# Four pairs of k tiles by seven products in gate and up, bank copies on ACT, and one sum of weights on GpSimd

## The chip, the cores and the metric

The kernel runs on one core of one Trainium2 chip. The metric is device time in microseconds of one execution, the median of several runs. The engines are PE (TensorE, matrix products), ACT (ScalarE), DVE (VectorE), POOL (GpSimd) and SP (SyncE, which here only issues DMAs). Every engine takes its own instructions in a fixed order and waits on semaphores for the others.

## The reference, cut to what matters

Two decoder layers on 256 tokens of width 2048: sparse attention in layer a, dilated window attention in layer b, both with attention to 256 memory tokens, and after each a SwiGLU feed-forward network (FFN) of width 5632. All inputs are float32. The change is in the FFN and in what prepares its input:

```python
D_MODEL, SEQ, D_FF = 2048, 256, 5632

def swiglu(h, w_gate, w_up, w_down):
    return (jax.nn.silu(h @ w_gate) * (h @ w_up)) @ w_down

# at the end of each layer
h = h + o                                    # output projection of the attention
return h + swiglu(rms_norm(h, norm_ffn), w_gate, w_up, w_down)
```

## The kernel before

**Precision.** Every product of two float32 matrices is made of three PE matmuls. ACT rounds an operand to a high part (`hi`, line 76) and DVE forms the low part as the difference (`lo`, line 77); `mm3` (lines 83 to 87) adds hi·hi, lo·hi and hi·lo into a PSUM bank of 128x512. Below, a *product* is one `mm3`: three matmuls of 128x128 by 128x512. Weights are split on the chip as they arrive: `whi`/`wlo` for a *plain* chunk (128x1024, line 105, three buffers each), `qhi`/`qlo` for a *quarter* (line 865, two buffers each).

**Pairs of k tiles by seven products.** A group of the FFN makes four banks: two token tiles by two column blocks of 512 (gate and up, or two blocks of down). Two k tiles and these two by two form a 2x2 by 2x2 block product, which needs eight products when done plainly. The kernel does it by the Winograd form of Strassen's scheme in seven. `NPR = 3` pairs (six k tiles) go this way in every group, the other k tiles are plain. For the three pairs together a quarter of the weights is one tile of 128x1536: q11, q12, q22, q21. Sums of activations are formed once, when the input is turned (`Paired.finish`, line 272, slots 4 to 7), sums of weights in every group by DVE (lines 886, 893, 901, 913).

**Steps of a group.** `Group.steps` (line 877) returns s0 to s6, one `product` (line 864) of a quarter or a sum of quarters each: s0 q11, s1 q11+q12, s2 q11+q12+q22, s3 q12+q22, s4 q21, s5 q21 plus the sum of three, s6 q22. Each step splits its quarter (ACT, then DVE) and issues one `mm3` for each pair. Between them `keep` (line 872) copies a bank to SBUF on ACT, and DVE adds such copies to banks (896, 898) or forms the remainder `rest` (904), which is added to the fourth bank at the end (line 980, or to `h` in line 1004). The quarters stand in four rotating buffers (line 860).

**Order of the work.** `run_groups` (line 939) writes PE's order by hand: the steps of the *next* group lie between the plain chunks of the *present* one. `spacing` (line 932) says how many plain chunks stand before each step: with ten plain chunks in a group 2, 1, 1, 2, 1, 2, 1. When the last plain chunk is issued, `done` reads the four banks: for gate and up `gate_up` (line 977: Silu on ACT, a product on DVE, then eight transposes on PE and splits in `heads`, issued some products later), for down an addition to `h`. ACT, DVE, SP and POOL are ordered by the scheduler of the language; only PE's order is fixed by the program. Bank 3 has one PSUM buffer, banks 0 to 2 have two (line 69).

**Groups.** An FFN has eleven gate-and-up groups of 16 k tiles; the first is wholly plain (64 products), the other ten have 21 + 40 = 61 products. They lie in portions of 4, 4 and 3 (line 26), each followed by two down groups (16, 16 and 12 k tiles); the last portion of layer b goes through `final` (line 1159) instead. So there are 20 paired gate-and-up groups and 10 paired down groups in all.

The input of the FFN is turned by `Paired.turn` (line 282) while `project_out` (line 812) runs. GpSimd raises to the power -1/2 in `finish_rstd` (line 213) and does little else.

Of the kernel before, what the change touches and what calls it, by code (L numbers as in the profile page):

```python
# [16 lines left out]
P = 128  # L17
# [9 lines left out]
NPR = 3  # L27
NSL = 8
NRK = KT - 2 * NPR
SW = NPR * NSL * P  # L30
XW = SW + NRK * T
QW = NPR * 512
WARM = 9
EPS = 1e-6
# [7 lines left out]
def decoder_trunk(ctx: ExitStack, tc: tile.TileContext, a: dict, out: bass.AP):  # L42
# [7 lines left out]
    work = ctx.enter_context(tc.tile_pool(name="work", bufs=1))  # L50
    work.tile([P, 20], F32, name="padw")
    phase = ctx.enter_context(ExitStack())
    aux_stack = ExitStack()
    fbufs = [1]
    fpool = mm_ps = aux_ps = mm_tags = None
# [132 lines left out]
    ac = phase.enter_context(tc.tile_pool(name="ac", bufs=1))  # L188
# [3 lines left out]
    peT = ac.tile([P, 2, 32], F32, name="peT")  # L192
    gbias = ac.tile([P, 36], F32, name="gbias")
    w2 = ac.tile([P, 2, 2, HD], F32, name="w2")
    ac.tile([P, 16], F32, name="pada")
# [20 lines left out]
    def square_sum(ssq, src):  # L216
        junk = work.tile([P, 512], F32, tag="rope2", name="junk")
        nc.scalar.activation(junk, src, AF.Square, accum_out=ssq)  # L218
# [31 lines left out]
    class Paired:  # L250
# [4 lines left out]
        def __init__(self, x, nk, gain=None, sums=True):  # L255
            self.gain, self.sums, self.nk = gain, sums, nk
            self.S = tuple(v[:, :SW].rearrange("p (q s t) -> p q s t", s=NSL, t=P) for v in x)
            self.R = tuple(v[:, SW:].rearrange("p (k t) -> p k t", t=T) for v in x)
            self.xs = [self.at(k) for k in range(nk)]

        def at(self, k):
            if k >= 2 * NPR:
                return cols(tuple(v[:, k - 2 * NPR, :] for v in self.R))
            return lambda tt: self.slot(k // 2, ((1, 0), (2, 3))[k % 2][tt])
# [4 lines left out]
        def new_f(self):  # L269
            return fpool.tile([P, 4, P], F32, tag="xf", name="xf", bufs=fbufs[0])  # L270

        def finish(self, q, f):
            split(self.S[0][:, q, :4, :], self.S[1][:, q, :4, :], f)
            if self.sums:
                s = fpool.tile([P, 4, P], F32, tag="xs", name="xs", bufs=1)
                nc.vector.tensor_sub(s[:, 0, :], f[:, 0, :], f[:, 3, :])
                nc.vector.tensor_sub(s[:, 2, :], f[:, 1, :], f[:, 0, :])
                nc.vector.tensor_sub(s[:, 1, :], s[:, 0, :], f[:, 1, :])
                nc.vector.tensor_add(s[:, 3, :], f[:, 2, :], s[:, 1, :])
                split(self.S[0][:, q, 4:, :], self.S[1][:, q, 4:, :], s)  # L280

        def turn(self, nb, k2):
            k = nb * 4 + k2 * 2
            if k >= 2 * NPR:
                to_xT(nb, k2, None, self.gain, tuple(v[:, k - 2 * NPR:k - 2 * NPR + 2, :].rearrange("p c t -> p (c t)") for v in self.R))
                return
# [3 lines left out]
            f = self.new_f()  # L290
            for i in range(2):
                nc.scalar.activation(f[:, i * 2:i * 2 + 2, :], ps[:, i * T:(i + 1) * T].rearrange("p (s t) -> p s t", t=P),
                                     AF.Copy, scale=self.gain(k + i))
            self.finish(k // 2, f)

        def heads(self, j, tok):

            np_ = min(max(NPR - 2 * j, 0), 2)
            fs = []

            def step(tt):
# [3 lines left out]
                pv = ps.rearrange("p (c t) -> p c t", t=P)  # L305
                for q in range(np_):
                    if tt == 0:
                        fs.append(self.new_f())
                    d = fs[q][:, 1:3, :] if tt == 0 else fs[q][:, 0:4:3, :]
                    nc.scalar.activation(d, pv[:, 2 * q:2 * q + 2, :], AF.Copy)  # L310
                    if tt == 1:
                        self.finish(2 * j + q, fs[q])
                if np_ < 2:
                    r0 = 4 * j + 2 * np_ - 2 * NPR
                    n = 4 - 2 * np_
                    d = tuple(v[:, r0:r0 + n, tt * P:(tt + 1) * P] for v in self.R)
                    split(d[0], d[1], pv[:, 2 * np_:, :])
# [132 lines left out]
    att = (p1, 2, 4)  # L450

# [148 lines left out]
    def compress(kv, toks):  # L600
# [30 lines left out]
        def turn():  # L631
# [4 lines left out]
            z = ac.tile([P, 2, 60], F32, tag="cz", name="cz", bufs=1)  # L636
            nc.scalar.activation(z.rearrange("p i m -> p (i m)"), tr[:, :120], AF.Copy)
            s = ac.tile([P, 2, 30], F32, tag="cs", name="csg", bufs=1)
# [173 lines left out]
    def project_out(name, nk, ready, gi):  # L812
        op = Paired(new_x(), KT, lambda k: gains[:, gi, k:k + 1])
# [25 lines left out]
    class Group:  # L839
# [3 lines left out]

        late = False

        def __init__(self, op, quarters, rest, done, rest_done=None):
# [3 lines left out]
            self.k0 = 0 if quarters is None else 2 * NPR  # L850
# [8 lines left out]
        def load(self, i):  # L859
            t = fq.tile([P, QW], F32, tag="quart", name=("q11", "q12", "q22", "q21")[i], bufs=4)  # L860
            nc.sync.dma_start(t, self.q[i])
            return t

        def product(self, b, s, t, side, start=False):
            hl = [fq.tile([P, QW], F32R, tag=n, name=n, bufs=2) for n in ("qhi", "qlo")]
            split(hl[0], hl[1], t)
            for q in range(NPR):
                mm3(self.bank[b], self.op.slot(q, s), tuple(v[:, q * 512:(q + 1) * 512] for v in hl),
                    start and q == 0, q == NPR - 1, True)
                side.tick()  # L870

        def keep(self, b):
            t = fq.tile([P, 512], F32, tag="keep", name="keep", bufs=3)
# [3 lines left out]
        def steps(self, side):  # L877
            def s0():
                self.q11 = self.load(0)
                self.new(0)  # L880
                self.product(0, 1, self.q11, side, True)
                self.p1 = self.keep(0)

            def s1():
                self.q12 = self.load(1)
                nc.vector.tensor_add(self.q11, self.q11, self.q12)
                self.new(2)
                self.product(2, 4, self.q11, side, True)
                self.p5 = self.keep(2)

            def s2():
                self.q22 = self.load(2)
                nc.vector.tensor_add(self.q11, self.q11, self.q22)
                b2 = self.new(1)
                self.product(1, 5, self.q11, side, True)
                nc.vector.tensor_add(b2, b2, self.p1)
# [3 lines left out]
            def s3():  # L900
                nc.vector.tensor_add(self.q12, self.q12, self.q22)
                self.product(1, 6, self.q12, side)
                self.r = fq.tile([P, 512], F32, tag="rest", name="rest", bufs=2)
# [4 lines left out]
            def s4():  # L908
                self.q21 = self.load(3)
                self.product(0, 2, self.q21, side)  # L910

            def s5():
                nc.vector.tensor_add(self.q21, self.q21, self.q11)
                self.product(1, 3, self.q21, side)

            def s6():
                self.product(2, 7, self.q22, side)

            return [s0, s1, s2, s3, s4, s5, s6]

        def plain(self, c, side):
            if c == 0:
                self.new(3)
            ws = load_w(self.rest[c], 512)
            last = c == len(self.rest) - 1
            k = self.k0 + c
            for b in ((3, 0, 1, 2) if last else (0, 1, 2, 3)):
                x = self.op.xs[k](b % 2)
                mm3(self.bank[b], x, ws[b // 2], c == 0 and (b == 3 or self.k0 == 0), last, True)
# [33 lines left out]
    def ffn(pre, op, f_r, last):  # L963
        gq, gs = a[pre + "_gu_q"], a[pre + "_gu_s"]
        groups = []
        for pi, (b0, b1) in enumerate(PORTIONS):
# [4 lines left out]
            def hop(pi=pi, nk=nk, final=final, hp=hp):  # L971
                if "op" not in hp:
                    x = pair(lambda i: fh.tile([P, XW], F32R, tag=("hThi", "hTlo")[i], name=("hThi", "hTlo")[i]))
                    hp["op"] = Paired(x, nk, sums=not (final and pre == "b"))
# [346 lines left out]
```

## Time and profile before

| | |
|---|---|
| median of 3 runs | 2042.54 us (2041.19 to 2043.21) |
| the profiled execution | 2041.91 us |
| its span, first to last instruction | 2040.1 us |
| mean granted TensorE clock | 0.998 |
| busy ACT, DVE, POOL | 58%, 80%, 1% |
| from HBM | 394.87 MB, mean 196 GB/s |

The profile is one execution taken by the hardware profiler. Its *groups* name an instruction by its line, its engine and its tiles (output, an arrow, inputs), with a count, the sum of busy time and the mean of one in ns. The *waits* say who waited for whom: total us, times, longest. The *timeline* has a start, a duration, the engine, the line and the tiles, and in brackets how long the engine had stood idle and whom it waited for. The duration of a PE matmul is modelled and overlaps the next one; what a matmul costs is read from the distance of the starts. A DMA's time runs from issue to landing.

### The profile page before, as it was taken

How to read it: one execution, taken by the hardware profiler on the slowest of the kernel's cores; microseconds unless marked ns; L12 is line 12 of the kernel's file. 1: busy time of each engine (PE TensorE's matmuls, PEld its weight loads, DVE VectorE, ACT ScalarE, POOL GpSimd, SP SyncE). 2: the span in 40 equal slices, each digit the busy share in tenths (PEclk: the TensorE clock that was granted, in tenths of full speed). 3: DMA queues.
4: the chain of work that ended last, by engine and by line, in shares of the span. 5: the costliest groups of instructions: out<-in, count | busy, mean ns of one | idle time of the engine just before them, and what ended most of it. 6: DMA issues, size and time to landing. Idle time of an engine off the chain costs nothing.

```text
span 2040.1 us, 25602 instructions
## 1 busy us (share of the span) xinstructions
PE 2020.5 (99%) x9417; PEld 1676.7 (82%) x9417; DVE 1641.4 (80%) x2118; ACT 1190.4 (58%) x1573; POOL 10.8 (1%) x32
## 2 busy tenths in 40 slices
PE   9999999999999999999999999999999999999998
PEld 7898888878888888888887888878888888888886
DVE  6767898678888888888887678778888888888755
ACT  7755566656555566555565555656555565655543
POOL 0000000000000000000000000000000000000000
PEclk9999999999999999999999999999999999999999
DMA  8767633566655656556663755476556655566464
GB/s 302 270 201 236 218 116 122 178 253 199 208 184 194 201 195 225 186 186 208 203 209 114 235 167 158 147 262 201 185 186 201 225 202 186 182 206 221 136 204 146
DMA packets 104541, 400.74 MB, mean 196 GB/s; under 512 B 12128, under 2 KB 12512, under 8 KB 104032
## 3 DMA queue, kind: packets, MB, share of 16 engines
q1 hardware_dynamic: 103392, 395.31, 58.5%
q0 software_dynamic: 736, 2.75, 0.4%
q8 instruction: 74, 1.21, 0.3%
q10 hardware_dynamic: 288, 1.05, 0.1%
q14 instruction: 51, 0.42, 0.1%
HBM read 394.87 MB, written 4.19 MB: 196 GB/s over the span
## 4 chain that ended last, share of the span: by engine, by line
PE 95%; DVE 2%; ACT 1%; issue 0%; DMA 0%; SPq 0%; DVEq 0%; POOLq 0%; POOL 0%; ACTq 0%
PE mm L85 30%; PE mm L87 30%; PE mm L86 30%; PE aux L304 1%; PE aux L226 1%; DVE wlo L77 1%; PE aux L87 1%; PE aux L86 1%; PE aux L85 1%; PE aux L339 0%; ACT whi L76 0%; PE cmp L625 0%; PE cmp L624 0%; DVE E L377 0%; DMA memT_raw<-in_memT_dram 0%
## 5 line engine op out<-in xcount | busy, mean ns | idle before, releaser
L76 ACT ACTIVATE whi<-raw 128x1024 fp32r<-128x1024 f32 (+1 forms) x476 | 498.4, 1047 | 502.5 <-PE mm L86 461.3
L77 DVE TENSOR_TENSOR wlo<-raw,whi 128x1024 fp32r<-128x1024 f32 (+1 forms) x476 | 573.1, 1205 | 203.9 <-ACT whi L76 202.6
L85 PE MATMUL mm<-whi,xhi 128*128 128x512 f32 (+1 forms) x1376 | 537.5, 391 | 2.9 <-ACT junk L218 1.1
L87 PE MATMUL mm<-wlo,xhi 128*128 128x512 f32 (+1 forms) x1376 | 530.5, 386 | 0.0
L86 PE MATMUL mm<-whi,xlo 128*128 128x512 f32 (+1 forms) x1376 | 529.7, 385 | 0.0
L77 DVE TENSOR_TENSOR qlo<-q,qhi 128x1536 fp32r<-128x1536 f32 x210 | 368.6, 1757 | 75.5 <-ACT qhi L76 74.2
L76 ACT ACTIVATE qhi<-q 128x1536 fp32r<-128x1536 f32 x210 | 311.8, 1486 | 137.8 <-PE mm L86 115.2
L87 PEld LDWEIGHTS mm<-wlo,xhi 128*128 128x128 f32 x1376 | 258.3, 188 | 52.6
L85 PEld LDWEIGHTS mm<-whi,xhi 128*128 128x128 f32 x1376 | 258.6, 188 | 51.0 <-issue 2.5
L86 PEld LDWEIGHTS mm<-whi,xlo 128*128 128x128 f32 x1376 | 258.8, 188 | 47.0
L85 PE MATMUL mm<-whi,hThi 128*128 128x512 f32 x464 | 182.0, 392 | 0.1
L86 PE MATMUL mm<-whi,hTlo 128*128 128x512 f32 x464 | 180.7, 389 | 0.9 <-DVE hTlo L77 0.9
L87 PE MATMUL mm<-wlo,hThi 128*128 128x512 f32 x464 | 180.8, 390 | 0.0
L87 PE MATMUL mm<-qlo,xhi 128*128 128x512 f32 x420 | 163.5, 389 | 0.0
L85 PE MATMUL mm<-qhi,xhi 128*128 128x512 f32 x420 | 163.5, 389 | 0.0
L86 PE MATMUL mm<-qhi,xlo 128*128 128x512 f32 x420 | 163.5, 389 | 0.0
L80 DVE SCALAR_TENSOR_TENSOR wlo<-raw,gains,whi 128x512 fp32r<-128x512 f32 x160 | 113.8, 747 | 47.0 <-ACT whi L79 46.8
L79 ACT ACTIVATE whi<-raw,gains 128x512 fp32r<-128x512 f32 x160 | 107.7, 716 | 58.9 <-PE mm L86 51.3
L85 PE MATMUL mm<-whi,ohi 128*128 128x512 f32 x256 | 102.7, 401 | 1.3 <-ACT whi L79 1.3
L86 PEld LDWEIGHTS mm<-whi,hTlo 128*128 128x128 f32 x464 | 87.2, 188 | 19.0 <-DVE hTlo L77 1.2
L85 PEld LDWEIGHTS mm<-whi,hThi 128*128 128x128 f32 x464 | 87.1, 188 | 18.1 <-ACT hThi L76 0.6
L87 PEld LDWEIGHTS mm<-wlo,hThi 128*128 128x128 f32 x464 | 87.1, 188 | 18.1
(279 smaller groups left out, 2480.0 us busy)
## 6 DMA issues: line engine op xcount, KB each, us to landing
raw<-in_a_gu_s_dram SPq DMA_DIRECT2D x100, 512.0 KB, 4.2
raw<-in_b_gu_s_dram SPq DMA_DIRECT2D x100, 512.0 KB, 3.6
q<-in_a_gu_q_dram SPq DMA_DIRECT2D x40, 768.0 KB, 5.4
q<-in_b_gu_q_dram SPq DMA_DIRECT2D x40, 768.0 KB, 5.7
raw<-in_a_dn_s_dram SPq DMA_DIRECT2D x52, 512.0 KB, 4.2
raw<-in_b_dn_s_dram SPq DMA_DIRECT2D x40, 512.0 KB, 4.3
q<-in_a_dn_q_dram SPq DMA_DIRECT2D x24, 768.0 KB, 5.7
raw<-in_a_w_out_dram SPq DMA_DIRECT2D x32, 512.0 KB, 3.6
```

The source lines that it names most:

```text
L76: nc.scalar.activation(hi, src, AF.Copy)
L77: nc.vector.tensor_sub(lo, src, hi.bitcast(F32))
L79: nc.scalar.activation(hi, src, AF.Copy, scale=gain)
L80: nc.vector.scalar_tensor_tensor(lo, src, gain, hi.bitcast(F32), op0=ALU.mult, op1=ALU.subtract)
L85: nc.tensor.matmul(o, l[0], r[0], start=start, stop=False, skip_group_check=more)
L86: nc.tensor.matmul(o, l[1], r[0], start=False, stop=False, skip_group_check=more)
L87: nc.tensor.matmul(o, l[0], r[1], start=False, stop=stop, skip_group_check=more)
L226: nc.tensor.transpose(ps[:, i * P:(i + 1) * P], s, ident)
L304: nc.tensor.transpose(ps[:, i * P:(i + 1) * P], tok[tt][:, i * P:(i + 1) * P], ident)
```

## The change

Gate and up take four pairs (`NPX = 4`) instead of three, so a group has 28 + 32 = 60 products, eight plain chunks, and quarters of 128x2048. Down stays at three pairs (`NPH = 3`).

- **Buffers of the quarters:** q11, q22 and q12 get one buffer each (`qa`, `qc`, `qb`), and q21 is loaded into the buffer of q12.
- **Steps:** the sums are accumulated in place. s4 is now the product of q22, s5 loads q21, has GpSimd add it to the sum of three, and makes that product; s6 is the product of q21.
- **Bank copies:** s0 writes bank 1, ACT copies it to bank 0, and s2 goes on accumulating in bank 1. The DVE addition of line 896 and one `keep` go. In gate and up `rest` is copied by ACT into bank 3 (`begin`) before the first plain chunk accumulates there; the addition of line 980 goes.
- **Spacing:** 2, 1, 1, 2, 0, 2, 0 plain chunks for groups of eight, other rows for 16, 10 and 6, and `done` comes before s5 where it came before s6.
- **Input and heads:** `finish` works on one or two pairs at a time and forms the sums in place; `heads` copies for two pairs at once.
- **Space:** `work` goes into the phase pools, `hb` has two buffers, `keep` two, `rest` one, and some small tiles move to another pool, with padding.

```diff
-NPR = 3
+NPX = 4
+NPH = 3
-QW = NPR * 512
+QW = NPX * 512
...
+        def finish(self, q, n, f):
+            def part(s):
+                d = tuple(v[:, q:q + n, s:s + 4, :].rearrange("p q s t -> p q (s t)") for v in self.S)
+                split(d[0], d[1], f.rearrange("p q s t -> p q (s t)"))
+            part(0)
             if self.sums:
-                s = fpool.tile([P, 4, P], F32, tag="xs", name="xs", bufs=1)
...
+                nc.vector.tensor_sub(f[:, :, 3, :], f[:, :, 0, :], f[:, :, 3, :])
+                nc.vector.tensor_sub(f[:, :, 0, :], f[:, :, 1, :], f[:, :, 0, :])
+                nc.vector.tensor_sub(f[:, :, 1, :], f[:, :, 3, :], f[:, :, 1, :])
+                nc.vector.tensor_add(f[:, :, 2, :], f[:, :, 2, :], f[:, :, 1, :])
+                part(4)
...
         def load(self, i):
-            t = fq.tile([P, QW], F32, tag="quart", name=("q11", "q12", "q22", "q21")[i], bufs=4)
+            n = self.op.npr * 512
+            t = fq.tile([P, QW], F32, tag=("qa", "qb", "qc", "qb")[i], name=("q11", "q12", "q22", "q21")[i])[:, :n]
             nc.sync.dma_start(t, self.q[i])
...
             def s0():
-                self.q11 = self.load(0)
-                self.new(0)
-                self.product(0, 1, self.q11, side, True)
-                self.p1 = self.keep(0)
+                self.qa = self.load(0)
+                self.new(1)
+                self.product(1, 1, self.qa, side, True)
+                nc.scalar.activation(self.new(0), self.bank[1], AF.Copy)
             def s1():
-                self.q12 = self.load(1)
-                nc.vector.tensor_add(self.q11, self.q11, self.q12)
+                self.qb = self.load(1)
+                nc.vector.tensor_add(self.qa, self.qa, self.qb)
                 self.new(2)
-                self.product(2, 4, self.q11, side, True)
+                self.product(2, 7, self.qa, side, True)
                 self.p5 = self.keep(2)
             def s2():
-                self.q22 = self.load(2)
-                nc.vector.tensor_add(self.q11, self.q11, self.q22)
-                b2 = self.new(1)
-                self.product(1, 5, self.q11, side, True)
-                nc.vector.tensor_add(b2, b2, self.p1)
+                self.qc = self.load(2)
+                nc.vector.tensor_add(self.qa, self.qa, self.qc)
+                self.product(1, 5, self.qa, side)
                 u2 = self.keep(1)
                 nc.vector.tensor_sub(self.bank[2], self.bank[2], u2)
             def s3():
-                nc.vector.tensor_add(self.q12, self.q12, self.q22)
-                self.product(1, 6, self.q12, side)
+                nc.vector.tensor_add(self.qb, self.qb, self.qc)
+                self.product(1, 4, self.qb, side)
...
             def s4():
-                self.q21 = self.load(3)
-                self.product(0, 2, self.q21, side)
+                self.product(2, 6, self.qc, side)
             def s5():
-                nc.vector.tensor_add(self.q21, self.q21, self.q11)
-                self.product(1, 3, self.q21, side)
+                self.qb = self.load(3)
+                nc.gpsimd.tensor_add(self.qa, self.qa, self.qb)
+                self.product(1, 3, self.qa, side)
             def s6():
-                self.product(2, 7, self.q22, side)
+                self.product(0, 2, self.qb, side)
...
+        def begin(self):
+            b = self.new(3)
+            self.held = self.r is not None and self.rest_done is None
+            if self.held:
+                nc.scalar.activation(b, self.r, AF.Copy)
...
-        base = {16: (3, 2, 2, 2, 2, 2, 2), 10: (2, 1, 1, 2, 1, 2, 1), 6: (1, 1, 1, 1, 0, 1, 1)}[n]
         if late:
-            base = (5, 0, 1, 1, 1, 1, 1)
+            return (4, 0, 1, 1, 0, 2, 0), n - 8
+        base = {16: (4, 2, 2, 3, 2, 3, 0), 10: (3, 1, 1, 2, 1, 2, 0), 8: (2, 1, 1, 2, 0, 2, 0), 6: (1, 1, 1, 1, 1, 1, 0)}[n]
...
             def gate_up(g, j, hop=hop, late=b1 - b0 < 4):
-                up = g.bank[3]
-                if g.r is not None:
-                    nc.vector.tensor_add(g.r, g.r, g.bank[3])
-                    up = g.r
...
-                    nc.vector.scalar_tensor_tensor(t, (g.bank[2], up)[tt], f_r[:, tt:tt + 1], t, op0=ALU.mult, op1=ALU.mult)
+                    nc.vector.scalar_tensor_tensor(t, g.bank[2 + tt], f_r[:, tt:tt + 1], t, op0=ALU.mult, op1=ALU.mult)
```

More of the change, by code (lines that the diff above doesn't have):

```diff
@@ L216, in square_sum @@
     def square_sum(ssq, src):
-        junk = work.tile([P, 512], F32, tag="rope2", name="junk")
+        junk = work.tile([P, 512], F32, tag="rope2", name="junk") if work is not fq else work.tile([P, 512], F32, tag="hb", name="junk", bufs=2)
         nc.scalar.activation(junk, src, AF.Square, accum_out=ssq)
@@ L250, in decoder_trunk, with __init__ @@
     class Paired:
[L255 to L258, printed above, removed]
+        def __init__(self, x, npr, nk, gain=None, sums=True):
+            self.npr, self.gain, self.sums = npr, gain, sums
+            sw = npr * NSL * P
+            self.S = tuple(v[:, :sw].rearrange("p (q s t) -> p q s t", s=NSL, t=P) for v in x)
+            self.R = tuple(v[:, sw:].rearrange("p (k t) -> p k t", t=T) for v in x)
             self.xs = [self.at(k) for k in range(nk)]
         def at(self, k):
-            if k >= 2 * NPR:
-                return cols(tuple(v[:, k - 2 * NPR, :] for v in self.R))
+            if k >= 2 * self.npr:
+                return cols(tuple(v[:, k - 2 * self.npr, :] for v in self.R))
             return lambda tt: self.slot(k // 2, ((1, 0), (2, 3))[k % 2][tt])
@@ L849, in __init__ @@
             self.r = None
[L850 removed]
+            self.plain_only = quarters is None
             if quarters is None:
@@ L864, in product @@
         def product(self, b, s, t, side, start=False):
-            hl = [fq.tile([P, QW], F32R, tag=n, name=n, bufs=2) for n in ("qhi", "qlo")]
+            npr = self.op.npr
+            hl = [fq.tile([P, QW], F32R, tag=n, name=n, bufs=2)[:, :npr * 512] for n in ("qhi", "qlo")]
             split(hl[0], hl[1], t)
-            for q in range(NPR):
+            for q in range(npr):
                 mm3(self.bank[b], self.op.slot(q, s), tuple(v[:, q * 512:(q + 1) * 512] for v in hl),
-                    start and q == 0, q == NPR - 1, True)
+                    start and q == 0, q == npr - 1, True)
                 side.tick()
         def keep(self, b):
-            t = fq.tile([P, 512], F32, tag="keep", name="keep", bufs=3)
+            t = fq.tile([P, 512], F32, tag="keep", name="keep", bufs=2)
             nc.scalar.activation(t, self.bank[b], AF.Copy)
@@ L972, in hop @@
                 if "op" not in hp:
-                    x = pair(lambda i: fh.tile([P, XW], F32R, tag=("hThi", "hTlo")[i], name=("hThi", "hTlo")[i]))
-                    hp["op"] = Paired(x, nk, sums=not (final and pre == "b"))
+                    x = pair(lambda i: fh.tile([P, HW], F32R, tag=("hThi", "hTlo")[i], name=("hThi", "hTlo")[i]))
+                    hp["op"] = Paired(x, NPH, nk, sums=not (final and pre == "b"))
                 return hp["op"]
             def gate_up(g, j, hop=hop, late=b1 - b0 < 4):
-                up = g.bank[3]
-                if g.r is not None:
-                    nc.vector.tensor_add(g.r, g.r, g.bank[3])
-                    up = g.r
                 hb = []
                 for tt in range(2):
-                    t = work.tile([P, 512], F32, tag="hb", name="hb", bufs=4)
+                    t = work.tile([P, 512], F32, tag="hb", name="hb", bufs=2)
                     nc.scalar.activation(t, g.bank[tt], AF.Silu, scale=f_r[:, tt:tt + 1])
-                    nc.vector.scalar_tensor_tensor(t, (g.bank[2], up)[tt], f_r[:, tt:tt + 1], t, op0=ALU.mult, op1=ALU.mult)
+                    nc.vector.scalar_tensor_tensor(t, g.bank[2 + tt], f_r[:, tt:tt + 1], t, op0=ALU.mult, op1=ALU.mult)
                     hb.append(t)
@@ L994, in ffn @@
                 else:
-                    groups.append(Group(op, [gq[b - 1, i] for i in range(4)], [gs[b - 1, c] for c in range(NRK)], done))
+                    groups.append(Group(op, [gq[b - 1, i] for i in range(4)], [gs[b - 1, c] for c in range(KT - 2 * NPX)], done))
             if final and pre == "b":
@@ L1014, in done @@
                                 nc.vector.tensor_add(hbk, ps[tt], hbk)
-                groups.append(Lazy(n2 == 0 and b1 - b0 < 4, hop, [dq[pi, n2, i] for i in range(4)], [ds[n2, c] for c in range(nk - 2 * NPR)], done, rest_done))
+                groups.append(Lazy(n2 == 0 and b1 - b0 < 4, hop, [dq[pi, n2, i] for i in range(4)], [ds[n2, c] for c in range(nk - 2 * NPH)], done, rest_done))
         run_groups(groups)
@@ L1280, in _layout @@
         gate, up, wd = i[pre + "_w_gate"][0], i[pre + "_w_up"][0], i[pre + "_w_down"][0]
-        q, r, first = _pairs(np, gate, up, NFB)
+        q, r, first = _pairs(np, gate, up, NFB, NPX)
         g[pre + "_gu_0"] = first
```

97 lines of the change are left out of this document (43 added, 54 removed).

## The prediction

> **What bounds the kernel now.** First the page: busy time by engine, and the chain of work that ended last.
>
> ```profile
> PE 2020.5 (99%) x9417; PEld 1676.7 (82%) x9417; DVE 1641.4 (80%) x2118; ACT 1190.4 (58%) x1573; POOL 10.8 (1%) x32
> ...
> PE 95%; DVE 2%; ACT 1%; issue 0%; DMA 0%; SPq 0%; DVEq 0%; POOLq 0%; POOL 0%; ACTq 0%
> ```
>
> PE carries 95% of the chain. A busy PE need not be at its peak, so next the waits, to see who is held up by whom.
>
> ```profile
> ACT whi L76 <- PE mm L86: 461.3, 322, 3.7
> DVE wlo L77 <- ACT whi L76: 202.6, 218, 3.3
> ACT qhi L76 <- PE mm L86: 115.2, 125, 1.0
> ```
>
> ACT waits for PE to give split buffers back, and DVE waits for ACT. Both run ahead of PE until buffers run out: PE is the bound, and its cost per product is what counts. From PE's timeline, two starts 28 products apart without a transpose between, and the same step (s1) of two gate-and-up groups in succession:
>
> ```profile
> 799.67 0.39 PE L85 MATMUL mm<-whi,xhi 128*128 128x512 f32 x1
> ...
> 818.71 0.39 PE L85 MATMUL mm<-whi,xhi 128*128 128x512 f32 x1
> ```
>
> ```profile
> 489.92 0.40 PE L87 MATMUL mm<-qlo,xhi 128*128 128x512 f32 x1
> ...
> 532.37 0.40 PE L87 MATMUL mm<-qlo,xhi 128*128 128x512 f32 x1
> ```
>
> A product (three matmuls) costs 19.04 / 28 = 0.680 us, not three times the modelled 0.39. A group takes 42.45 us: 61 products are 41.48, so its eight transposes take 0.97.
>
> **The change: what PE saves.** Each of 20 groups goes from 61 to 60 products: 20 x 0.680 = **13.6 us** less. Nothing else on PE changes in number. The profiled execution took 2041.9 us, 0.6 below the median; if PE stays the bound it becomes 2028.3. A group then takes PE 60 x 0.680 + 0.97 = 41.77.
>
> **What ACT and DVE pay.** The groups by shape:
>
> ```profile
> L76 ACT ACTIVATE whi<-raw 128x1024 fp32r<-128x1024 f32 x460 | 487.8, 1061 | 488.3 <-PE mm L86 448.4 <-issue 12.3 <-ACT qhi L76 5.7
> L76 ACT ACTIVATE qhi<-q 128x1536 fp32r<-128x1536 f32 x210 | 311.8, 1486 | 137.8 <-PE mm L86 115.2 <-DVE q L893 15.0 <-DVE q L913 3.8
> ...
> L874 ACT ACTIVATE keep<-mm 128x512 f32<-128x512 f32 x90 | 52.9, 588 | 29.9 <-PE mm L87 28.1 <-DVE mm L896 1.3
> ```
>
> ```profile
> L77 DVE TENSOR_TENSOR wlo<-raw,whi 128x1024 fp32r<-128x1024 f32 x460 | 561.4, 1222 | 192.3 <-ACT whi L76 191.0 <-PE cmp L625 0.7
> L77 DVE TENSOR_TENSOR qlo<-q,qhi 128x1536 fp32r<-128x1536 f32 x210 | 368.6, 1757 | 75.5 <-ACT qhi L76 74.2
> ...
> L913 DVE TENSOR_TENSOR q<-q,q 128x1536 f32<-128x1536 f32 x30 | 52.5, 1751 | 0.0
> ...
> L896 DVE TENSOR_TENSOR mm<-mm,keep 128x512 f32<-128x512 f32 x30 | 20.8, 695 | 0.0
> ```
>
> ```profile
> 755.00:797.00 42.00, 42.00 (x191) 34.76 (x190) 38.73 (x38) 25.22 (x29) 0.00 (x0) 1.00 0.59 202
> ```
>
> From 1024 to 1536 columns ACT adds 0.425 and DVE 0.535, so at 2048 ACT's split takes 1.91 and DVE's split or sum 2.29. DVE in a group: two splits less (-2.44), one sum less (-1.75), line 896 and its like in 980 gone (-1.39), ten instructions longer (+5.35): -0.2, no gain. ACT: -2.12, +2.98, and one bank copy more (+0.59): +1.4. The last row (a busy stretch of 42 us: PE, PEld, DVE, ACT) shows 25.2 of ACT and 38.7 of DVE: ACT's extra hides in idle time (28 us over 20 groups if that were gone), DVE stays close under PE. The copy from bank 1 to bank 0 has three steps of PE (8.2 us) before PE writes bank 1 again: nothing.
>
> **Where the cover gets thin: the buffers.** Before, four buffers rotated and q11 came early. Now q21 goes into the buffer that s3 just read, and the next q11 into the one that s5 just read. That closes a loop, from s3's low part to the next group's: load q21, GpSimd sum, split; load q11, split; two sums and two splits in turn, then s3's split. GpSimd's price is the unknown one. Its rows, and those of the loads:
>
> ```profile
> L649 POOL MEMSET E<- 128x384 f32 x1 | 0.4, 420 | 105.7 <-PE aux L635 105.7
> masks.py:199 POOL TENSOR_SCALAR_AFFINE_SELECT ident<-ident 128x128 f32<-128x128 f32 x1 | 0.3, 294 | 0.1
> masks.py:197 POOL MEMSET ident<- 128x128 f32 x1 | 0.2, 205 | 0.3 <-POOLq L1316 0.3
> ```
>
> ```profile
> q<-in_a_gu_q_dram SPq DMA_DIRECT2D x1, 768.0 KB, 4.3
> q<-in_a_gu_q_dram SPq DMA_DIRECT2D x1, 768.0 KB, 5.7
> ```
>
> ```profile
> h<-in_x_dram SPq DMA_DIRECT2D x2, 1024.0 KB, 8.6
> ```
>
> ```profile
> GB/s 302 270 201 236 218 116 122 178 253 199 208 184 194 201 195 225 186 186 208 203 209 114 235 167 158 147 262 201 185 186 201 225 202 186 182 206 221 136 204 146
> ```
>
> The memsets give 0.84 ns per column written and 0.10 us fixed; the select, one read and one write, 1.53 ns. For 2048 columns that is 3.2 us with one read, and 4.7 if a second read costs as much as the first (0.69 ns). These are the ends; I take the middle, **3.9**, since the add reads twice but nothing shows that reads don't overlap. The two q loads are those of steps that now close the loop (q21 after SP had waited: 4.3; q11: 5.7). 256 KB more at the highest 302 GB/s of a slice are 0.87: 5.2 and 6.6, and 8.6 is the upper end, `h`'s load of that size.
>
> The Trainium skill, "GPSIMD Engine Reference", section 3.1, gives 4497 ns for just this add at 2048 columns and 2293 for DVE, and says to leave elementwise work to DVE; the 2293 agrees with 2.29 here. By its 4.5 the sum below would come to 2040, not 2031.
>
> The rest of the loop, from DVE's timeline: s0's split at 770.27, the first sum at 774.40, s2's split ending at 786.04, s3's split at 789.52, in a window with the heavier kind of heads.
>
> ```profile
> 770.27 1.76 DVE L77 TENSOR_TENSOR qlo<-q,qhi 128x1536 fp32r<-128x1536 f32 x1
> ...
> 773.27 1.22 DVE L77 TENSOR_TENSOR wlo<-raw,whi 128x1024 fp32r<-128x1024 f32 x1
> 774.40 1.75 DVE L886 TENSOR_TENSOR q<-q,q 128x1536 f32<-128x1536 f32 x1
> ...
> 786.04 0.69 DVE L77 TENSOR_TENSOR hTlo<-xf,hThi 128x512 fp32r<-128x512 f32 x1
> ...
> 787.79 1.22 DVE L77 TENSOR_TENSOR wlo<-raw,whi 128x1024 fp32r<-128x1024 f32 x1
> 788.92 0.68 DVE L77 TENSOR_TENSOR hTlo<-xs,hThi 128x512 fp32r<-128x512 f32 x1
> 789.52 1.75 DVE L77 TENSOR_TENSOR qlo<-q,qhi 128x1536 fp32r<-128x1536 f32 x1
> ```
>
> From the end of s0's split (772.03) to that of s3's (791.27) is 19.24. Six instructions get 0.535 longer (+3.21); what lies before the chunk's split at 773.27, the products of `gate_up` (1.24), and that split (1.13) now fall into the wait for q11: 20.1. Without the heads at 786.04 to 787.79 and 788.92 to 789.52 it is 17.7.
>
> | part of the loop | takes | PE meanwhile |
> |---|---|---|
> | s3 to s5: 5.2 + 3.9 + 1.91 + 2.29 | 13.3 | s3, s4, two chunks: 10.88 |
> | s5 to next s0: 6.6 + 1.91 + 2.29 | 10.8 | s5, s6, two chunks, half the transposes: 11.37 |
> | s0 to s3 | 20.1, light 17.7 | s0 to s2, four chunks, half the transposes: 19.53 |
> | sum | 44.2, light 41.8 | 41.77 |
>
> So a window with heavy heads falls behind by 2.43 us, a light one by nothing. It starts with a reserve: s3's split may run at most 7.1 us ahead of PE (its buffer comes free 10.88 before; less 4.20, plus 0.45 for the two matmuls that need no low part). At s2, where it is tightest, 3.8 of these are needed: 13.3 + 10.8, then 13.8 to the end of s2's split (14.01 in the rows, 2.14 longer, 2.37 moved), less PE's 22.25 + 11.37 + 0.45. 3.3 are left. Down groups refill it. A portion of four has one light and two heavy windows: 4.86 - 3.3 = 1.6 us of waiting; a portion of three, one of each: none. Two FFNs: 3.1. **Forecast: 2041.9 - 13.6 + 3.1 = 2031.** With GpSimd at 3.2 the waits vanish (2028); at 4.7 they are 15.6 (2044).
>
> Small edits: bank 3 is now free only after both products of line 986 (1.24 above), but s5 and s6 (5.4 us of PE) cover that and the copy. One pair more in each `project_out` gives DVE the work seen at 786.04 to 789.52 twice, off the path; 7 us if it were on it. The new waits have others behind them: on SP the chunk loads behind q21 (four `raw` buffers hold 10.9 us of PE ahead), on ACT the split of s6 and two chunks behind that of s5 (three `whi` buffers), on POOL nothing. Each is covered unless q21 comes more than some 5 us late. The short down groups of layer a (45 products, 30.6 us) may wait up to 3 us once; I take nothing.
>
> **The rivals.**
>
> *The saving is given back* by a slower add. If the loop is e longer than summed, waits grow by four windows' worth in the portion of four (three windows, and the reserve shrinks too) and three in each other: 10e per FFN, 20e in all, less 0.4. At e = 0.7 us they eat the 13.6: 2042. For: GpSimd at 4.7 alone gives e = 0.8. Against: q21 landed in 4.3 when alone.
>
> *Slower: GpSimd and DVE hold each other up.* The place is between s3 and s5; almost all of DVE's work there reads two SBUF tiles, as does the add. If an add must let a split finish first (1.22) and otherwise costs 3.9 to 4.7, e is 1.2 to 2.0, 2052 to 2068, with the middle at 2060; it decides from e = 0.7. Nothing in this trace shows GpSimd beside a busy DVE. The Trainium skill, "SBUF — State Buffer", section "Who interferes with whom", says that a DVE instruction with two SBUF inputs and a GpSimd one that reads SBUF exclude each other, the later one blocked until the first ends; no run here shows it yet. Against: DVE is idle for much of the wait for q21.
>
> *Slower: late loads.* With h's 8.6 instead of 5.2 in a third of the windows e averages 1.1: 2050.
>
> *It does not shorten PE's list*: excluded by the count above.
>
> **How the numbers follow.** Forecast case (2027 to 2038): 0.48. Given back (2038.5 to 2046.6, which is 0.2% around the median and about what a measurement can tell from no change): 0.16. Blocked GpSimd or DVE: 0.24. Late loads: 0.12. So faster 0.48, same 0.16, slower 0.36. The range goes from just below the sum without waits (2027) to e = 1.7 (2062), which leaves out a third of the slower cases and little else. The forecast's own range is 2027 to 2038.
>
> **What would show it.** Right: 60 matmuls fewer on PE; 40.8 us plus transposes per gate-and-up window; PE's waits under 10 us in all; the add under 4.5 us. Wrong: PE waiting for `qhi` or `qlo` at s5, s0, s1 or s2, more in the second and third window of a portion than in the first (the loop); adds of 5 us or more, or splits of DVE above 2.3 us while an add runs (the port); loads of q21 over 6 us (late loads).

## The result, and the profile after

The changed kernel takes 2070.36 us, median of 4 runs (2067.04 to 2072.32), against 2042.88 for the kernel before on the same chip: a ratio of 1.0138, 95% interval 1.0126 to 1.0150. The forecast was 2031, with a range up to 2062. The profiled execution took 2067.04 us, its span is 2065.2 and its mean granted clock 0.993 (0.998 before).

The page of the changed kernel, busy time by engine, and the chain that ended last:

```profile
PE 2022.1 (98%) x9357; PEld 1669.1 (81%) x9357; DVE 1715.4 (83%) x1975; ACT 1213.9 (59%) x1534; POOL 147.5 (7%) x62
...
PE 79%; DVE 11%; DMA 4%; ACT 3%; issue 2%; POOL 1%; SPq 0%; POOLq 0%; DVEq 0%; ACTq 0%
```

PE has the 60 matmuls fewer that were counted, but its part of the chain fell from 95% to 79%. DVE has 143 instructions fewer and is busy 74 us longer. The groups by shape, columns as before, say which:

```profile
L77 DVE TENSOR_TENSOR wlo<-raw,whi 128x1024 fp32r<-128x1024 f32 x420 | 599.9, 1433 | 129.8 <-ACT whi L76 126.3 <-PE aux L290 2.2 <-PE cmp L628 0.7
L77 DVE TENSOR_TENSOR qlo<-q,qhi 128x2048 fp32r<-128x2048 f32 x140 | 322.9, 2315 | 65.3 <-ACT qhi L76 65.1
...
L917 POOL TENSOR_TENSOR q<-q,q 128x2048 f32<-128x2048 f32 x20 | 101.4, 5071 | 797.1 <-DMA q<-in_a_gu_q_dram 362.0 <-DMA q<-in_b_gu_q_dram 320.4 <-DVE mm L902 77.1
L917 POOL TENSOR_TENSOR q<-q,q 128x1536 f32<-128x1536 f32 x10 | 35.3, 3529 | 358.4 <-DMA q<-in_a_dn_q_dram 214.7 <-DMA q<-in_b_dn_q_dram 143.7
```

The mean split of a chunk is 1433 ns where it was 1222, and GpSimd's add takes 5071. The timeline shows the two together (start, duration, engine, line, tiles; in brackets the idle time before):

```profile
722.65 1.21 DVE L77 TENSOR_TENSOR wlo<-raw,whi 128x1024 fp32r<-128x1024 f32 x1
722.65 5.68 POOL L917 TENSOR_TENSOR q<-q,q 128x2048 f32<-128x2048 f32 x1 [38.43 <-DMA q<-in_a_gu_q_dram]
724.43 4.99 DVE L77 TENSOR_TENSOR wlo<-raw,whi 128x1024 fp32r<-128x1024 f32 x1 [0.57 <-ACT whi L76]
```

A split that begins while the add runs takes 4.99 us. The add ends at 728.33, the split at 729.42, 1.09 later, which is about a split's own time: it waited for the add. The first split, which starts in the same hundredth of a microsecond as the add, kept its 1.21, and this add is among the longer ones. Over the twenty adds of this size, the five that begin with at most 0.11 us of a split left on DVE take 4.60 to 4.62 us, the six that begin with 1.07 to 1.22 us of one left take 5.54 to 5.69. So each waits for the other, whichever comes second. The Trainium skill, "SBUF — State Buffer", section "Who interferes with whom", says that these two exclude each other; the rows agree. The Trainium skill, "GPSIMD Engine Reference", section 3.1, has 4497 ns for this add; here the shortest takes 4.60 us and the mean is 5.07, beside a busy DVE.

The chain of waits of the changed kernel in the same window shows the loop of single buffers closed, from s3's low part to s2's of the next group (pieces under 0.1 us are left out):

```profile
715.42 2.30 DVE qlo L77
717.74 4.75 DMA q<-in_a_gu_q_dram
722.65 5.69 POOL q L917
728.37 1.93 ACT qhi L76
730.32 2.30 DVE qlo L77
732.64 4.76 DMA q<-in_a_gu_q_dram
737.50 1.93 ACT qhi L76
739.46 2.30 DVE qlo L77
...
755.56 2.21 DVE qlo L77
757.81 0.50 PE mm L87
```

PE's last matmul of a product (line 87) starts when s2's low part is ready: PE follows the loop here. Its wait is short in this window, 0.22 us; over the three windows of this portion, PE's waits for s2's low part are 0.27, 0.22 and 1.99 us, the longest in the last, which is what the prediction named as the sign of the loop. PE's waits over the whole span:

```profile
PE mm L87 <- DVE qlo L77: 11.7, 12, 2.0
PE mm L85 <- DVE mm L902: 3.7, 2, 2.2
PE aux L224 <- DVE xlo L80: 3.5, 2, 2.1
PE mm L86 <- DVE hTlo L77: 2.8, 2, 1.4
...
PE mm L85 <- ACT xf L293: 1.7, 1, 1.7
```

The first row is the loop's, the others are not. But the second is GpSimd's too: one of its two waits ends at 1069.59, in the steps of a short down group, where line 902 stands on DVE behind a split that an add holds up.

```profile
1063.80 3.52 POOL L917 TENSOR_TENSOR q<-q,q 128x1536 f32<-128x1536 f32 x1 [38.33 <-DMA q<-in_a_dn_q_dram]
1063.98 4.94 DVE L77 TENSOR_TENSOR qlo<-q,qhi 128x1536 fp32r<-128x1536 f32 x1 [1.26 <-ACT qhi L76]
1068.85 0.69 DVE L902 TENSOR_TENSOR mm<-mm,keep 128x512 f32<-128x512 f32 x1
```

Where the waits lie is seen from an instruction that stands at the same point of the program in both kernels, the sum of squares at the end of `project_out` (first and third row) and of the FFN of layer a (second). DVE's timeline, before and then after:

```profile
420.19 0.16 DVE L208 TENSOR_REDUCE var<-ssq 128x2 f32<-128x8 f32 x1
1124.27 0.16 DVE L208 TENSOR_REDUCE var<-ssq 128x2 f32<-128x8 f32 x1 [0.94 <-ACT junk L218]
1330.20 0.16 DVE L208 TENSOR_REDUCE var<-ssq 128x2 f32<-128x8 f32 x1
```

```profile
419.53 0.16 DVE L206 TENSOR_REDUCE var<-ssq 128x2 f32<-128x8 f32 x1
1140.21 0.16 DVE L206 TENSOR_REDUCE var<-ssq 128x2 f32<-128x8 f32 x1 [0.70 <-ACT junk L216]
1347.69 0.16 DVE L206 TENSOR_REDUCE var<-ssq 128x2 f32<-128x8 f32 x1
```

The differences of these starts, up to the end of the span, for this kernel and those of the experiments (us, one profiled execution each):

| kernel | FFN a | attention b and projection | FFN b |
|---|---|---|---|
| before | 704.1 | 205.9 | 709.9 |
| before less ten products (6.8) in each FFN | 697.3 | 205.9 | 703.1 |
| after | 720.7 | 207.5 | 717.5 |
| `sum_dve` | 714.8 | 207.5 | 710.4 |
| `sum_qc` | 708.6 | 207.4 | 710.9 |
| `pool_qc` | 710.5 | 207.5 | 710.4 |
| `qc_late16` | 706.5 | 207.4 | 705.9 |
| `qc_best` | 705.7 | 206.5 | 708.4 |
| `qc_ticks` | 702.0 | 206.5 | 706.4 |

A profiled execution lies up to 6 us from the median of its kernel (that of `sum_dve`, 2054.1, was the slowest of eight), so the table says where time is lost rather than how much.

### The profile page after: what moved, and what is told of

Its sections match the earlier page's. It is cut to its first block, busy times and chain, and to the rows that moved or that the text cites. A ratio compares the mean times of both kernels' runs of the same rounds, so it can differ in the third digit from the quotient of the medians.

```text
span 2065.2 us, 25244 instructions
## 1 busy us (share of the span) xinstructions
PE 2022.1 (98%) x9357; PEld 1669.1 (81%) x9357; DVE 1715.4 (83%) x1975; ACT 1213.9 (59%) x1534; POOL 147.5 (7%) x62
## 4 chain that ended last, share of the span: by engine, by line
PE 79%; DVE 11%; DMA 4%; ACT 3%; issue 2%; POOL 1%; SPq 0%; POOLq 0%; DVEq 0%; ACTq 0%
PE mm L87 25%; PE mm L85 25%; PE mm L86 25%; DVE qlo L77 4%; DVE wlo L77 3%; ACT qhi L76 2%; DMA q<-in_a_gu_q_dram 2%; DVE q L899 1%; POOL q L917 1%; DMA q<-in_b_gu_q_dram 1%; PE aux L224 1%; PE aux L87 1%; DVE hTlo L77 1%; PE aux L86 1%; PE aux L85 1%
## 5 line engine op out<-in xcount | busy, mean ns | idle before, releaser
L77 DVE TENSOR_TENSOR qlo<-q,qhi 128x2048 fp32r<-128x2048 f32 (+1 forms) x210 | 450.8, 2155 | 102.3 <-ACT qhi L76 100.8
L76 ACT ACTIVATE qhi<-q 128x2048 fp32r<-128x2048 f32 (+1 forms) x210 | 371.0, 1774 | 257.2 <-PE mm L86 93.4
L85 PE MATMUL mm<-whi,xhi 128*128 128x512 f32 (+1 forms) x1216 | 477.2, 392 | 3.7 <-ACT xf L293 1.7
L87 PE MATMUL mm<-wlo,xhi 128*128 128x512 f32 (+1 forms) x1216 | 469.6, 386 | 0.0
L86 PE MATMUL mm<-whi,xlo 128*128 128x512 f32 (+1 forms) x1216 | 469.0, 386 | 0.0
L87 PE MATMUL mm<-qlo,xhi 128*128 128x512 f32 x560 | 220.9, 394 | 11.7 <-DVE qlo L77 11.7
L917 POOL TENSOR_TENSOR q<-q,q 128x2048 f32<-128x2048 f32 (+1 forms) x30 | 136.7, 4557 | 1155.5 <-DMA q<-in_a_gu_q_dram 362.0
L87 PEld LDWEIGHTS mm<-qlo,xhi 128*128 128x128 f32 x560 | 105.6, 189 | 39.5 <-DVE qlo L77 17.4
L85 PEld LDWEIGHTS mm<-qhi,xhi 128*128 128x128 f32 x560 | 105.7, 189 | 25.4 <-ACT qhi L76 2.2
L86 PEld LDWEIGHTS mm<-qhi,xlo 128*128 128x128 f32 x560 | 105.6, 189 | 22.2
```

The costliest lines, as they stand in the source:

```text
L76: nc.scalar.activation(hi, src, AF.Copy)
L77: nc.vector.tensor_sub(lo, src, hi.bitcast(F32))
L85: nc.tensor.matmul(o, l[0], r[0], start=start, stop=False, skip_group_check=more)
L86: nc.tensor.matmul(o, l[1], r[0], start=False, stop=False, skip_group_check=more)
L87: nc.tensor.matmul(o, l[0], r[1], start=False, stop=stop, skip_group_check=more)
L917: nc.gpsimd.tensor_add(self.qa, self.qa, self.qb)
```

## The experiments

All edits are to the changed kernel, but for one to the kernel before. The kernel before took 2041.5 to 2042.5 beside them. The medians:

| run | us | ratio to before, 95% interval |
|---|---|---|
| after | 2070.36 | 1.0138 (1.0126 to 1.0150) |
| `sum_dve` | 2048.24 | 1.0034 (1.0022 to 1.0047) |
| `pool_aside` | 2075.60 | 1.0159 (1.0142 to 1.0176) |
| `loop_longer` | 2060.59 | 1.0089 (1.0069 to 1.0108) |
| `before_pool` | 2042.77 | 1.0006 (0.9997 to 1.0015) |
| `sum_qc` | 2047.48 | 1.0025 (1.0015 to 1.0035) |
| `pool_qc` | 2051.23 | 1.0042 (1.0029 to 1.0056) |
| `qc_late16` | 2043.57 | 1.0004 (0.9995 to 1.0013) |
| `pool_memset` | 2047.62 | 1.0027 (1.0016 to 1.0037) |
| `npx3_pool` | 2044.56 | 1.0019 (1.0010 to 1.0028) |
| `qc_best` | 2043.77 | 1.0013 (1.0004 to 1.0022) |
| `qc_ticks` | 2037.97 | 0.9983 (0.9974 to 0.9992) |

### GpSimd's sum: the loop, or DVE being held?

**`sum_dve`**, the fourth sum back on DVE:

```diff
-                nc.gpsimd.tensor_add(self.qa, self.qa, self.qb)
+                nc.vector.tensor_add(self.qa, self.qa, self.qb)
```

> The changed kernel, with the fourth sum on DVE instead of GpSimd. Loop theory (what costs is the time round the loop of the single buffers, q21 into q12's buffer and the next q11 into the sum's): the sum takes 2.3 us in place of 5.1, the loop gets 2.8 us shorter, and most of the 39 us of waits go: 2028 to 2038. Port theory (what costs is that GpSimd's add and DVE's splits shut each other out): DVE's 102 us of lengthened instructions go, the chunk splits are back at 1.22 us in the mean, and 63 us of sums come: the same 2028 to 2038. A third theory (bank copies, the copy of the remainder or the new order cost it): no less than 2060.

22.1 us go, the split of a chunk is back at its time, and PE no longer waits for line 902. But both theories had 2028 to 2038, and the third no less than 2060; 2048 lies between. It is still above the kernel before, and some 20 above the 2028 that was expected without waits: the add is about half of what was lost.

```profile
L77 DVE TENSOR_TENSOR wlo<-raw,whi 128x1024 fp32r<-128x1024 f32 x420 | 511.4, 1219 | 127.0 <-ACT whi L76 123.4 <-PE aux L290 2.2 <-PE cmp L628 0.7
```

**`pool_aside`**, as `sum_dve`, and GpSimd adds q22's buffer to itself after s4's last use of it, so that it reads beside DVE without forming the sum. Nothing reads what it writes:

```diff
                 self.product(2, 6, self.qc, side)
+                nc.gpsimd.tensor_add(self.qc, self.qc, self.qc)
```

> As sum_dve, and after s4 GpSimd adds the q22 tile to itself, 30 adds of the same size as in the changed kernel that nothing in the loop waits for (only the next load of q22, which is early). Loop theory: as sum_dve within 3 us. Port theory: chunk splits of DVE up to 5 us long again, mean above 1.35 us, and the time 10 to 35 us above sum_dve.

**`loop_longer`**, as `sum_dve`, and GpSimd fills q21's buffer before q21 is loaded (1816 ns, written only):

```diff
+                nc.gpsimd.memset(self.qb, 0.0)
                 self.qb = self.load(3)
```

> As sum_dve, and GpSimd writes zeros over the q12 buffer between its last read in s3 and the load of q21: the loop gets longer by a memset (1.4 to 1.8 us by the memset rows, at 0.84 ns per column), and GpSimd reads nothing. Loop theory: at 20 us per us of loop beyond the reserve, 10 to 35 us above sum_dve; DVE's splits keep 1.22 us. Port theory: as sum_dve within 3 us.

**`before_pool`**, the kernel before with line 913 on GpSimd:

```diff
-                nc.vector.tensor_add(self.q21, self.q21, self.q11)
+                nc.gpsimd.tensor_add(self.q21, self.q21, self.q11)
```

> The kernel before (three pairs, four rotating buffers, no tight loop) with its fourth sum, line 913, on GpSimd. Loop theory: no difference from the kernel before, 2040 to 2045. Port theory: DVE is relieved of 52 us of sums but held for 30 adds of 3.5 us; chunk splits above 1.3 us in the mean; the time is no better, 2043 to 2060.

**`pool_memset`**, as `pool_aside`, but GpSimd only writes:

```diff
+                nc.gpsimd.memset(self.qc, 0.0)
```

> The kernel with the sum by DVE, and after the product of q22 (s4) GpSimd fills the buffer of q22 with zeros instead of adding it to itself as in the run with GpSimd's add set aside. The next load of q22 waits for GpSimd in both. Theory that GpSimd's reading of SBUF holds DVE up: splits of weights stay at 1220 ns and the time stays near that of the kernel with the sum by DVE, 2046 to 2052. Rival, the wait of the load of q22 for GpSimd is what cost 27 us there: 2065 to 2076.

The chunk splits of `pool_aside` and of `pool_memset`, with GpSimd's own group:

```profile
L77 DVE TENSOR_TENSOR wlo<-raw,whi 128x1024 fp32r<-128x1024 f32 x420 | 587.2, 1401 | 115.9 <-ACT whi L76 112.5 <-PE aux L290 2.2 <-PE cmp L628 0.7
L914 POOL TENSOR_TENSOR q<-q 128x2048 f32<-128x2048 f32 x20 | 78.4, 3919 | 827.2 <-DVE qlo L77 827.2
...
L899 DVE TENSOR_TENSOR q<-q,q 128x2048 f32<-128x2048 f32 x20 | 45.7, 2283 | 0.0
```

```profile
L77 DVE TENSOR_TENSOR wlo<-raw,whi 128x1024 fp32r<-128x1024 f32 x420 | 511.7, 1221 | 126.9 <-ACT whi L76 123.4 <-PE aux L290 2.2 <-PE cmp L628 0.7
L914 POOL MEMSET q<- 128x2048 f32 x20 | 36.3, 1816 | 843.4 <-DVE qlo L77 843.4
```

GpSimd holds DVE up when it reads (1401 ns), not when it only writes (1221). The Trainium skill, "SBUF — State Buffer", section "Who interferes with whom", has it so too. `pool_memset` costs nothing over `sum_dve`, `pool_aside` 27.4 us. The load of the next q22 waits 2.1 us longer for the add than for the fill, but that is not the loss: DVE never stands idle before line 899, the first to read q22 (0.0 in the last row of the first view), and ACT waits for no chunk of the FFN's weights. The length of the loop counts too: `loop_longer` leaves the chunk splits at 1220 ns and costs 12.4 us, 6.8 for each us of loop (a rough figure, from four runs between 2056 and 2064). In `before_pool` DVE is held as well, with splits of 1394 ns, and the time does not change. So the hold alone is not the loss. That kernel differs in two things, four rotating buffers and three pairs; `npx3_pool` below takes them apart.

**`sum_qc`** and **`pool_qc`** test that from the other side. The sum is written into q22's buffer, free since s4's split, so that q11's buffer is free as soon as the sum is formed and not only after s5's split. In `pool_qc` the sum is GpSimd's:

```diff
-                nc.gpsimd.tensor_add(self.qa, self.qa, self.qb)
-                self.product(1, 3, self.qa, side)
+                nc.vector.tensor_add(self.qc, self.qa, self.qb)
+                self.product(1, 3, self.qc, side)
```

> The changed kernel with the fourth sum by DVE, written into the buffer of q22 instead of over the sum of three, and the product of s5 taken from there. So the next group's q11 may be loaded as soon as the sum is formed, without waiting for s5's split (1.91 + 2.29 = 4.2 us less in the loop of single buffers). Theory of the loop: the five to six us that the kernel with the sum by DVE still waits in its gate-and-up windows go: 2041 to 2044, with PE's waits for qlo at half or less. Rival, the chain of sum and split on a nearly full DVE from s0 to s2 sets those waits: no change, 2046 to 2050. By either, what is lost outside these windows (13 us between the last down group of layer a and the first gate-and-up groups, by the comparison of the traces) stays.

> The same as the kernel with the sum in q22's buffer, but the sum by GpSimd. The loop is shorter than in the changed kernel by the same 4.2 us, while GpSimd and DVE still meet. Theory that DVE is held for as long as an add runs: splits of weights near 1400 ns in the mean as in the changed kernel, and most of GpSimd's loss stays: 10 us or more above the kernel with the sum in q22's buffer by DVE, 2053 to 2065. Rival, GpSimd costs only through the length of the loop: within 4 us of that kernel.

| fourth sum by | over the sum of three | in q22's buffer |
|---|---|---|
| GpSimd | 2070.4 | 2051.2 |
| DVE | 2048.2 | 2047.5 |

With the sum over the sum of three GpSimd costs 22.1 us, with 4.2 us taken out of the loop 3.8. In `pool_qc` the rival has the time right and the theory the splits: DVE is held as in the changed kernel, and yet nearly all of the loss is gone. Nor is it that DVE is full: it is busy 1715.4 us in the changed kernel and 1714.3 in `pool_qc`, 19 us faster.

```profile
L77 DVE TENSOR_TENSOR wlo<-raw,whi 128x1024 fp32r<-128x1024 f32 x420 | 612.9, 1464 | 128.6 <-ACT whi L76 124.9 <-PE aux L290 2.2 <-PE cmp L628 0.7
L917 POOL TENSOR_TENSOR q<-q,q 128x2048 f32<-128x2048 f32 x20 | 99.9, 4996 | 792.7 <-DMA q<-in_b_gu_q_dram 319.7 <-DMA q<-in_a_gu_q_dram 241.5 <-DVE mm L902 80.1
```

Against `sum_dve` its chunk splits take 101 us more (612.9 - 511.4), and the time is 3.0 us more. For DVE's sum the shorter loop brings 0.8 us, as the rival had it, and not the 4 to 7 of the loop theory, although PE's waits for `qlo` fall from 6.4 to 3.3 us: what `sum_dve` lost was mostly elsewhere.

**`npx3_pool`**, all of the change but the fourth pair:

```diff
-NPX = 4
+NPX = 3
```

> The changed kernel with three pairs in gate and up instead of four, and all else of the change: single buffers, the fourth sum by GpSimd, bank copies by ACT. A quarter is 128x1536 again, so each load, sum and split in the loop of buffers is a quarter shorter (GpSimd's add 3.53 instead of 5.07 us), and a group has 61 products. Theory that the loop of single buffers with GpSimd's add in it is too long only at the width of four pairs: 2042 to 2048, PE's waits for qlo a few us in all. Rival, the buffers, the copies or GpSimd cost at any width: 2055 or more.

2044.56, as expected: by the interval of its ratio, single buffers, bank copies and GpSimd's sum cost 2 to 6 us at three pairs. DVE is held here too, with chunk splits of 1387 ns, and PE has no wait for `qlo`. So the short buffers do not make the loss by themselves either; the loop is too long only at the width of four.

### The other 20 us

Against its second row, the table by stretches puts 17.5 us of `sum_dve`'s loss in the FFN of layer a, 1.6 in the projection of layer b and 7.3 in the FFN of layer b; for `sum_qc` they are 11.3, 1.5 and 7.8. The largest single wait of `sum_dve` is where the first FFN starts, seen in its timeline:

```profile
425.02 1.91 ACT L76 ACTIVATE qhi<-q 128x2048 fp32r<-128x2048 f32 x1 [2.84 <-DMA q<-in_a_gu_q_dram]
...
426.84 0.46 ACT L79 ACTIVATE xhi<-aux,gains 128x256 fp32r<-128x256 f32 x1
426.97 2.29 DVE L77 TENSOR_TENSOR qlo<-q,qhi 128x2048 fp32r<-128x2048 f32 x1 [3.49 <-ACT qhi L76]
...
429.18 0.48 DVE L80 SCALAR_TENSOR_TENSOR xlo<-aux,gains,xhi 128x256 fp32r<-128x256 f32 x1
...
429.80 1.09 PE L224 MATMUL aux<-ident,h 128*128 128x128 f32 x4 [4.29 <-DVE xlo L80]
```

ACT stands at the split of the first q11, which is a third larger than before and has not landed (2.84 us). Behind it on ACT and DVE stand the splits of the last turn, `xhi` and `xlo`; these must read the one bank of transposes before PE can write the next four there. So PE waits 4.29 us for a load that it needs only later. How late this load is differs between executions: ACT waits 0.69 us for it in the profile of the changed kernel and 1.85 in that of `sum_qc`, and PE then 2.14 and 3.30. Some 1.45 us of PE's wait remain in each; in the kernel before it was 0.47 in all.

**`qc_late16`**, as `sum_qc`, with s0 after six plain chunks of the first group; q12 is then loaded two chunks after q11 and not right behind it:

```diff
-        base = {16: (4, 2, 2, 3, 2, 3, 0), ...
+        base = {16: (6, 2, 2, 2, 2, 2, 0), ...
```

> The kernel with the sum in q22's buffer by DVE, and in the first, wholly plain group of each network s0 after six plain chunks instead of four. Theory: the 3 to 7 us lost twice at the start of the network come from the first q11, which lands with q12 on its heels after 7.9 us and holds up ACT, behind whose split stands the turn that PE waits for; with q12 loaded two chunks later and the turn ahead of the split PE waits there under 1 us: 6 to 13 us below the kernel with the sum in q22's buffer. Rival, the fourth pair's own work in the turn is what costs: no change, within 2 us.

3.9 us, between the two theories: ACT waits 0.66 us for q11 where it was 1.85 in `sum_qc`, but its split still stands ahead of the turn's, and PE's waits for `xlo` are 3.4 us in two places (4.6 in `sum_qc`). At the start of the second FFN PE's waits at the first s0, 0.72 us for `qhi` and 1.59 for `qlo`, are gone as well.

**`qc_best`**, as `qc_late16`, with the two edits below. **`qc_ticks`**, as `qc_best`, with the second half of the last turn three products later:

```diff
-            f = fpool.tile([P, 1, 4, P], F32, tag="xf", name="xf")
+            f = fpool.tile([P, 1, 4, P], F32, tag="xf", name="xf", bufs=2)
...
-                deferred.extend(at(hop().heads(j, hb), *((4, 10) if late and j == 1 else (6, 14))))
+                deferred.extend(at(hop().heads(j, hb), *((4, 10) if late else (6, 14))))
```

```diff
-            residual_block(ps, nb, ssq, op, (3, 5) if nb == 2 else (4, 10))
+            residual_block(ps, nb, ssq, op, (3, 5) if nb == 2 else (4, 13))
```

> The kernel with the sum in q22's buffer by DVE and the late first s0, with two edits at the places where its trace still loses to the one before: a second buffer for the float copy of the turn (xf) in the output projection, for which PE's transposes wait 1.7 us there, and the last heads of the portion of three four and two products earlier, whose high and low part PE waits for by 0.8 and 1.4 us in the short down group, with some 4 us of half clock behind. Theory that these are the places where the saving of four pairs is lost: 2036 to 2041. Rival, the waits move to the next late tile: 2042 to 2045.

> The last kernel, and the second half of the last turn three products later, where PE waits 2.1 and 1.3 us for the low part of the first half to release the one bank of transposes. Theory: those waits and their half clock go: 3 to 6 us below the last kernel, 2032 to 2038. Rival, the low part stands behind the split of q11 on DVE however late the transposes are, and moves with them: within 2 us.

`qc_best` is no faster than `qc_late16`: the wait for `xf` goes (206.5 for the stretch, after 207.5), but the waits for `xlo` grow from 3.4 to 6.0 us, so the rival was right there. `qc_ticks` takes most of these away and is 5.8 us faster than `qc_best`, part of which only undoes what `qc_best` had made worse; its waits for the two tiles:

```profile
PE mm L87 <- DVE qlo L77: 2.8, 8, 0.5
...
PE aux L224 <- DVE xlo L80: 0.6, 1, 0.6
```

At 2037.97 it is the one version here that is faster than both kernels: 0.9983 of the time before, interval 0.9974 to 0.9992. Four pairs pay, by a little, without GpSimd's sum, with the sum in q22's buffer and four more edits outside the products of a group (the late s0, the buffer of `xf`, the heads and the turn); which of them are needed was not tried.

## Why the prediction was wrong

**What PE saves: right, but not to be had alone.** The 60 matmuls are gone, and from s0 of one group to s0 of the next PE takes 41.88 and then 42.31 us (the low products of s0 start at 704.18, 746.06 and 788.37 in the profile after) where the prediction had 41.77. `qc_ticks` reaches 702.0 and 706.4 in the FFNs where 697.3 and 703.1 stand for the full saving: 5.6 of the 13.6 us are there.

**GpSimd's add: the step that failed first.** The prediction took 3.9 us, with 4.7 as the upper end; it takes 5.07 in the mean, above both, beside a DVE that it holds up and that holds it up. Of the 1.17 us too much, 0.70 are the add itself (4.60 at its shortest) and some 0.47 the splits that it waits for. The 0.70 alone is the point from which the prediction's rival decides. By the prediction's own formula e = 1.17 costs 20 x 1.17 = 23 us; taking the add away brought 22.1. That these agree is partly luck: the formula knows neither the held splits nor the clock (last section), PE's waits for `qlo` come to 11.7 us and not 23, and where the length of the loop alone was changed (`loop_longer`) it cost 6.8 us for each us and not 20. The rival "GpSimd and DVE hold each other up" was the true course, with a chance, 0.24, that was too low. That its price (2052 to 2068) came so near 2070 is luck too, since some 20 us of the 42 lost have other causes. The chance stayed small because nothing in the trace of before showed GpSimd beside DVE, though the rule named there spoke for it. The argument against, that DVE idles in the wait for q21, fails in the rows: a chunk's split begins 1.78 us after the add does and is held.

**The loop: the right structure, with terms that cancelled.**

| part (us) | predicted | chain of after, one window |
|---|---|---|
| s3 to s5 | 13.3 | 14.9 |
| s5 to s0 | 10.8 | 9.1 |
| s0 to the end of s2's split | 13.8 | 16.0 |

q11 landed in 4.76 us, not 6.6, which gave back the longer add. The third part was the worse one: other splits stand ahead of s2's on DVE, more than the rows of before showed. The sum up to s2 is 40.0 instead of 37.9, and of the reserve of 7.1 us it needs 6.0 in one window and not 3.8.

**Edits costed at nothing: the other half.** `sum_dve` still stands 20 us above 2028. The prediction put "one pair more in each `project_out`" off the path, 7 us if it were on it, and gave the first load of an FFN no thought; loading q12 and starting s0 later there brought 3.9 us (`qc_late16`), and the turn's second half later 5.8, of which some undoes `qc_best` (`qc_ticks`). The short down groups were allowed up to 3 us and given nothing; the waits for `hTlo` are there, but `qc_best` did not show their price by itself. The wait for line 902 in the steps of one is the held split's, and GpSimd's. In the trace of before PE waits for `xlo` 0.5 us at most: that the place was already without slack could be read there.

**Bank copies by ACT: right.** ACT is busy 23.5 us longer, and no chain or wait shown here ends on a bank copy; they were not taken away alone.

**Late loads: no, but for the first.** In the window shown q21 and q11 landed in 4.75 and 4.76 us, and in all twenty gate-and-up windows the add starts 4.9 to 5.9 us after the load of q21 is issued; what came late was the first q11 of an FFN, a place that this rival didn't name.

**What stays open.** `qc_ticks` is still 9 us above 2042.5 - 13.6 = 2028.9; PE's waits in its trace sum to 15.4 us (9.9 before), and where the rest is was not tried. How much of the 22.1 us is the add's own length and how much the splits held behind it was not separated: `loop_longer` has the length without the hold and `pool_aside` the hold without the length, but both beside a sum by DVE, and together they cost more than 22.1. At `loop_longer`'s 6.8 us for each us of loop, the 2.8 us by which the add exceeds DVE's sum would be 19, an estimate.

## What to carry to other kernels

Before handing an idle engine work, look at what it shares: here a GpSimd add that reads SBUF stopped DVE instructions that read two tiles. Price that by what waits for the add and for DVE and not by busy time: it cost 22 us on a loop of single buffers at four pairs, 3.8 with that loop 4.2 us shorter, 2 to 6 (with the bank copies and new order in it) on single buffers at three pairs, and nothing with four rotating buffers at three pairs. When a sum is formed in place, ask which operand is needed back first and write to the one that isn't; for GpSimd's sum this one line was worth 19 us, for DVE's 0.8. And look at the first use of a larger tile: a load that comes late there blocks the engine's queue, and with it work that has nothing to do with it.

## What was not expected of the hardware

A wait of PE can cost more than its length. The windows of the changed kernel around the wait of 2.17 us for line 902 that ends at 1069.59 (columns: length, PE busy and matmuls, granted clock, share and rate of the DMAs):

```profile
1063.59:1069.59 6.00, 3.83 (x18) 1.00 0.26 89
1069.59:1075.59 6.00, 6.00 (x19) 0.72 0.75 249
1075.59:1081.59 6.00, 6.00 (x28) 1.00 0.89 311
```

The mean clock of the 6 us behind it is 0.72, which is 1.7 us lost, and 19 matmuls start where 28 do a little later. Over the span the clock went from 0.998 to 0.993, some 10 us of 2065, beside PE's waits, whose sum over all rows went from 9.9 to 33.7 us. The Trainium skill, "TensorE: Matmul & The Clock Gate", Part 1, has the clock fall to half after an idle window of some 3.4 us; here a wait of 2.17 us was enough. Length alone does not decide it in this trace: PE waits 1.99 us for `qlo` four times, and the 6 us behind show a clock of 0.72 twice (at 802.23 and 1476.19) and of 1.00 twice (at 548.42 and 1733.67).
